# Stores moved to a second DMA ring, issued by ScalarE ten tiles behind the results

## The chip, the cores and the metric

One Trainium2 chip, one of its cores. The metric is the device time of one execution in microseconds (us); a median of several executions is quoted. Engine names: TensorE (PE) does matmuls, VectorE (DVE) and ScalarE (ACT) elementwise work, SyncE (SP) issues transfers. A transfer that SyncE or ScalarE issues is put in that engine's own ring (queues q1 and q10 on the pages below), a waiting list of transfers; 16 DMA engines take work from the rings. PSUM is the memory that TensorE writes its results to.

## The reference

```python
batch, m, k, n = 16, 512, 1024, 768
x          # (16, 512, 1024) float32
weight     # (1024, 768)     float32
sub_value  # (16, 512, 768)  float32
return (np.matmul(x, weight) - sub_value).astype(np.float32)
```

The 8192 rows of x are cut into 64 tiles of 128 rows ("m tiles"). Per tile 512 KB of x and 384 KB of sub_value are loaded and 384 KB of result are stored. With 3 MB of weight that is 87 MB in all.

## The kernel before

Two ring buffers live in on-chip memory: `x_ring` holds 16 tiles of x, `so_ring` holds 32 tiles of sub_value, in which the results replace what was subtracted. ScalarE casts a tile of x to 16 bits; TensorE transposes it (and ScalarE copies it out of PSUM), or, for the pairs of tiles in `ON_DVE`, VectorE transposes it; then TensorE multiplies, and VectorE subtracts. Tiles transposed by VectorE are cast seven tiles ahead of their matmuls, the others four.

All transfers are in one hand-ordered list, and SyncE issues them in that order: `x`, `w`, `s` are loads of x, weight and sub_value, `o` is a store; the numbers are the first tile and how many.

```python
TRANSFERS = [
    # ... the first 18 entries cut ...
    ('x', 27, 5), ('o', 0, 8), ('s', 24, 8), ('x', 32, 8), ('s', 32, 8), ('o', 8, 8),
    ('x', 40, 8), ('s', 40, 8), ('x', 48, 8), ('o', 16, 8), ('o', 24, 8), ('s', 48, 8),
    ('x', 56, 8), ('s', 56, 8), ('o', 32, 8), ('o', 40, 8), ('o', 48, 8), ('o', 56, 4),
    ('o', 60, 2), ('o', 62, 1), ('o', 63, 1),
]

def issue():                       # called after each cast and each subtraction
    while todo:
        kind, at, n = todo[0]
        # ... return if a buffer is not yet free, or a result not yet there (cut) ...
        todo.pop(0)
        # ...
        if kind == "o":
            keep(nc.sync.dma_start(out=there, in_=here))
        else:
            keep(nc.sync.dma_start(out=here, in_=there))

for mi in range(HEAD, n_mt):
    # ... matmuls of tile mi, transposes of tile mi + 2 (cut) ...
    for t in range(mi, n_mt):
        if t - lead(t) == mi:      # lead is 7 for tiles transposed by VectorE, else 4
            cast(t)
    finish(mi)                     # the subtraction
```

ScalarE runs its instructions in the order of the program, so a cast that waits for its load holds up everything behind it there. A load of sub_value into a place of `so_ring` must wait until the old result there has been stored. And in a single ring the list decides whose bytes move first: the transfers of the kernel before landed in the order of its list.

## Time and profile before

| | before |
|---|---|
| median time | 211.19 us of 3 runs, later 211.16 of 4 |
| span in the profile | 209.4 us |
| TensorE busy | 198.4 us |
| DMA engines busy | 97.7% of the span |
| bytes moved | 87.03 MB, 417 GB/s |
| last subtraction done, last store landed | 205.4, 208.5 us |

Read it from the outside in: two resources are above 90%, so first ask which of them the end hangs on (the chain that ended last says TensorE), then what the other one would do if it were a little later.

### The profile page before, as it was taken

How to read it: one execution, taken by the hardware profiler on the slowest of the kernel's cores; microseconds unless marked ns; L12 is line 12 of the kernel's file. 1: busy time of each engine (PE TensorE's matmuls, PEld its weight loads, DVE VectorE, ACT ScalarE, POOL GpSimd, SP SyncE). 2: the span in 40 equal slices, each digit the busy share in tenths (PEclk: the TensorE clock that was granted, in tenths of full speed). 3: DMA queues.
4: the chain of work that ended last, by engine and by line, in shares of the span. 5: the costliest groups of instructions: out<-in, count | busy, mean ns of one | idle time of the engine just before them, and what ended most of it. 6: DMA issues, size and time to landing. Idle time of an engine off the chain costs nothing.

```text
span 209.4 us, 2967 instructions
## 1 busy us (share of the span) xinstructions
PE 198.4 (95%) x1249; PEld 130.4 (62%) x1249; DVE 114.1 (54%) x186; ACT 112.6 (54%) x115; POOL 0.7 (0%) x6
## 2 busy tenths in 40 slices
PE   7998789999979999999999999999999999999990
PEld 2464467676656576676666666667666766766660
DVE  0342044206149849929946965992994795332231
ACT  3555565675396183655727629355573760765410
POOL 1000000000000000000000000000000000000000
PEclk9999999999999999999999999999999999999999
DMA  6999999999999999999999999999999999999994
GB/s 221 420 426 424 424 438 439 433 443 426 391 455 415 442 427 423 454 413 432 435 421 449 423 413 444 451 418 421 418 441 440 423 437 418 426 446 427 415 383 167
DMA packets 5629, 87.22 MB, mean 417 GB/s; under 512 B 624, under 2 KB 624, under 8 KB 2032
## 3 DMA queue, kind: packets, MB, share of 16 engines
q1 hardware_dynamic: 5616, 87.03, 97.7%
q8 instruction: 10, 0.16, 0.3%
q14 instruction: 3, 0.02, 0.0%
HBM read 61.87 MB, written 25.17 MB: 416 GB/s over the span
## 4 chain that ended last, share of the span: by engine, by line
PE 68%; DMA 20%; ACT 4%; DVE 3%; SPq 1%; issue 1%
PE psum_o L177 60%; DMA x_ring<-in_x_dram 20%; PE psum_t L144 8%; ACT x_tile L135 2%; DVE xtp_tile L165 2%; ACT xt_tile L151 1%; DVE so_ring L189 1%; SPq L110 1%; SPq L122 1%; ACT x16p_tile L132 0%
## 5 line engine op out<-in xcount | busy, mean ns | idle before, releaser
L177 PE MATMUL psum_o<-w_sb,xt_tile 128*128 128x384 f16 x800 | 145.7, 326 | 1.7 <-ACT xt_tile L151 1.1
L177 PEld LDWEIGHTS <-xt_tile 128*128 128x128 f16 x800 | 78.2, 98 | 41.5 <-ACT xt_tile L151 1.9
L189 DVE TENSOR_TENSOR so_ring<-psum_o,so_ring 128x768 f32<-128x768 f32 x64 | 60.7, 957 | 61.2 <-PE psum_o L177 41.1
L151 ACT COPY xt_tile<-psum_t 128x1024 f16<-128x1024 f16 x50 | 50.6, 1012 | 75.7 <-PE psum_t L144 74.9
L165 DVE STREAM_TRANSPOSE xtp_tile<-x16p_tile 32x256 f32<-32x256 f32 x112 | 48.8, 436 | 18.9 <-ACT x16p_tile L132 17.2
L144 PE MATMUL psum_t<-ident,x_tile 128*128 128x128 f32 x200 | 52.5, 275 | 2.8 <-ACT x_tile L135 2.4
L135 ACT CAST x_tile<-x_ring 128x1024 f16<-128x1024 f32 x50 | 51.6, 1049 | 5.5 <-DMA x_ring<-in_x_dram 5.5
L177 PE MATMUL psum_o<-w_sb,xtp_tile 128*128 128x384 f16 x224 | 42.9, 326 | 0.3 <-DVE xtp_tile L165 0.3
L144 PEld LDWEIGHTS psum_t<-ident,x_tile 128*128 128x128 f32 x200 | 27.8, 142 | 16.8 <-ACT x_tile L135 4.7
L177 PEld LDWEIGHTS <-xtp_tile 128*128 128x128 f16 x224 | 21.8, 98 | 10.4 <-DVE xtp_tile L165 0.7
L132 ACT CAST x16p_tile<-x_ring 128x1024 f16<-128x1024 f32 x14 | 14.6, 1046 | 5.8 <-DMA x_ring<-in_x_dram 4.7
L205 PE MATMUL psum_o<-idle_x,idle_w 128*128 128x512 f16 x25 | 8.8, 508 | 1.3 <-DVE idle_x L200 1.3
L112 DVE CAST w_sb<-so_ring 128x768 f16<-128x768 f32 x8 | 4.1, 556 | 10.5 <-DMA so_ring<-in_weight_dram 10.5
L205 PEld LDWEIGHTS <-idle_w 128*128 128x128 f16 x25 | 3.0, 120 | 5.0 <-issue 3.2
L135 ACT ACT_TABLE_LOAD x1 | 1.3, 1283 | 0.7 <-PEq L277 0.7
L199 DVE MEMSET idle_w<- 128x64 uint32 x1 | 0.1, 112 | 0.8 <-PEq L277 0.8
masks.py:199 POOL TENSOR_SCALAR_AFFINE_SELECT ident<-ident 128x128 f32<-128x128 f32 x1 | 0.3, 292 | 0.1
L200 DVE MEMSET idle_x<- 128x256 uint32 x1 | 0.3, 272 | 0.0
masks.py:197 POOL MEMSET ident<- 128x128 f32 x1 | 0.2, 205 | 0.3 <-POOLq L277 0.3
L277 POOL MEMSET const-bfloat16-1.0<- 128x1 bf16 x1 | 0.1, 101 | 0.0
L277 POOL MEMSET const-uint8-127<- 128x1 uint8 x1 | 0.1, 101 | 0.0
L277 POOL MEMSET const-float32-0.0<- 128x1 f32 x1 | 0.1, 98 | 0.2 <-issue 0.2
(1 smaller groups left out, 0.1 us busy)
## 6 DMA issues: line engine op xcount, KB each, us to landing
so_ring<-in_sub_value_dram SPq DMA_DIRECT2D x7, 3072.0 KB, 24.2
out_dram<-so_ring SPq DMA_DIRECT2D x7, 3072.0 KB, 31.2
x_ring<-in_x_dram SPq DMA_DIRECT2D x5, 4096.0 KB, 22.3
x_ring<-in_x_dram SPq DMA_DIRECT2D x2, 2560.0 KB, 23.3
x_ring<-in_x_dram SPq DMA_DIRECT2D x3, 1536.0 KB, 19.8
so_ring<-in_weight_dram SPq DMA_DIRECT2D x4, 768.0 KB, 8.7
x_ring<-in_x_dram SPq DMA_DIRECT2D x3, 512.0 KB, 6.2
so_ring<-in_sub_value_dram SPq DMA_DIRECT2D x1, 1536.0 KB, 22.2
```

Of the source, the lines that this page charges most:

```text
L110: keep(nc.sync.dma_start(out=st, in_=w_c[at]))
L112: keep(nc.vector.tensor_copy(out=w_sb[:, at, r], in_=st[:, r]))
L122: keep(nc.sync.dma_start(out=here, in_=there))
L132: keep(nc.scalar.copy(out=x16_t["pair", first][:, mi - first], in_=x_in))
L135: keep(nc.scalar.copy(out=x16_t[mi], in_=x_in))
L144: keep(nc.tensor.transpose(ps_t[mi].bitcast(F32)[:, c * P : (c + 1) * P], x16_t[mi].bitcast(F32)[:, c * P : (c + 1) * P], ident,))
L151: keep(nc.scalar.copy(out=xt_t[mi], in_=ps_t.pop(mi)))
L165: keep(nc.vector.transpose(xt[b * Q : (b + 1) * Q, :, a * Q : (a + 1) * Q], x16[a * Q : (a + 1) * Q, :, b * Q : (b + 1) * Q],))
L177: keep(nc.tensor.matmul(po_t[mi][:, h, :NS], xt_t[mi][:, 2 * P * c + r : 2 * P * (c + 1) : 2], w_sb[:, c, r, h * NS : (h + 1) * NS], start ...
L189: keep(nc.vector.tensor_tensor(out=o, in0=po_t.pop(mi)[:, :, :NS], in1=o, op=mybir.AluOpType.subtract))
L205: keep(nc.tensor.matmul(idle_o[:, 0], idle_w, idle_x, start=True, stop=True))
L277: nc = _bacc.Bacc("TRN2", target_bir_lowering=False, num_devices=1)
```

## The change

The intent is that the 16 DMA engines take from two rings at once: loads stay on SyncE's, stores go to ScalarE's. So that ScalarE need not wait for a subtraction before it can issue a store, each store is issued about ten tiles after its last result was due (tiles 0 to 7 after tile 18, for instance); near the end it trails by less.

```diff
-TRANSFERS = [
+LOADS = [
     # ... (loads in the same order, the 'o' entries taken out)
 ]
+STORES = [(18, 0, 8), (26, 8, 8), (34, 16, 8), (42, 24, 8), (50, 32, 8), (54, 40, 8),
+          (58, 48, 8), (61, 56, 4), (63, 60, 2), (63, 62, 1), (63, 63, 1)]
 ...
+    def store(at, n):
+        assert set(range(at, at + n)) <= done["finish"]
+        done["o"] |= set(range(at, at + n))
+        keep(nc.scalar.dma_start(
+            out=out_s[at // S][:, at % S : at % S + n], in_=so_ring[:, at % NSO : at % NSO + n]
+        ))
+        issue()
 ...
         del waiting[:PER]
+        for after, at, n in STORES:
+            if after == mi:
+                store(at, n)
```

An entry (34, 16, 8) means: after tile 34's part of the program, store the 8 tiles from 16 on.

## The prediction

> **What bounds the kernel now.** I read the page's busy shares first, then the 40 slices, the DMA queues, the chain that ended last, the queue's own waits, and last the trace's record of when each transfer was issued and landed.
>
> ```profile
> PE 198.4 (95%) x1249; PEld 130.4 (62%) x1249; DVE 114.1 (54%) x186; ACT 112.6 (54%) x115; POOL 0.7 (0%) x6
> ...
> DMA  6999999999999999999999999999999999999994
> ...
> q1 hardware_dynamic: 5616, 87.03, 97.7%
> ...
> PE 68%; DMA 20%; ACT 4%; DVE 3%; SPq 1%; issue 1%
> ```
>
> Two resources are full at once: TensorE is busy for 198.4 of 209.4 us, and one queue keeps the 16 DMA engines busy for 97.7% of the span. The chain ends on TensorE: from 70.7 us to 204.5 us it is an unbroken run of matmuls and transposes, then one subtraction of 0.96 us, then the last store, issued at 205.5 and landed at 208.5. All gaps of TensorE together are 4.8 us, all but about 0.3 us of them before 60 us. So nothing that touches only transfers after 60 us can shorten the TensorE part; it can only keep it or delay it.
>
> The transfers have no spare rate either. Landings follow each other like this: a 3 MB load or store (8 tiles of 384 KB, 3.146 million bytes) every 7.23 to 7.33 us, so 429 to 435 GB/s, and a 4 MB x load every 9.7 us, 432 GB/s. Loads and stores cost the same per byte. By tile, x, sub_value and output together are 1280 KB, 3.03 us of DMA at 432 GB/s, while TensorE takes about 2.89 us per tile (subtraction of tile 25 at 97.0 us, of tile 49 at 166.4: 69.4/24). DMA is therefore the slower of the two in steady state, and TensorE is never starved after 60 us only because the list of transfers puts urgent loads ahead and lets stores pile up: the last load lands at 177.9 us, and 12.6 MB of stores follow it.
>
> How tight this is shows on ScalarE and in the queue's waits:
>
> ```profile
> 122.21 1.04 ACT L132 CAST x16p_tile<-x_ring 128x1024 f16<-128x1024 f32 x1 [1.50 <-DMA x_ring<-in_x_dram]
> ...
> 139.22 1.05 ACT L132 CAST x16p_tile<-x_ring 128x1024 f16<-128x1024 f32 x1 [1.17 <-DVE xtp_tile L165]
> 143.33 1.01 ACT L151 COPY xt_tile<-psum_t 128x1024 f16<-128x1024 f16 x1 [3.07 <-PE psum_t L144]
> ```
>
> ```profile
> SPq L122 <- ACT x_tile L135: 75.2, 7, 22.4
> SPq L120 <- DVE so_ring L189: 47.0, 6, 20.9
> SPq L122 <- DMA out_dram<-so_ring: 46.9, 4, 24.4
> ```
>
> The first fence is ScalarE's timeline: the cast of tile 42 waited for x(40..47), which landed at 122.14, and the cast of tile 48 began at 139.22, 0.08 us after x(48..55) landed at 139.14. The view names VectorE, whose transposes free the buffer at about the same moment, but the load leaves no margin either. The second is what the sequencer of SyncE waits for: buffers to be free and results to be done. Those waits cost nothing now, because a deep backlog stands in the ring meanwhile.
>
> **What the Trainium skill says.** "DMA: Bandwidth & Descriptors", section "Issuing engines are not separate DMA queues": transfers issued from ScalarE and SyncE run on the same 16 engines, and issuing from several saves only the sequencer's issue time. Here an issue is 0.33 to 0.47 us, 39 times, and hidden. The same page, "Where 436 GB/s comes from", gives 435 GB/s as the ceiling of the fabric; the trace, at 429 to 435, agrees and leaves nothing for a second ring to fill. The same page, "Queues, rings and completion order", says that each engine goes round robin between rings that have work, packet by packet. The trace before has one data ring, so it shows this only faintly: the ten 16 KB packets of the instruction queue took 1.00 to 1.10 us each, against 0.63 us at the 26 bytes per ns of the data queue's packets, so they shared their engine.
>
> **The change part by part.**
> 1. Issues move: 11 stores at about 0.4 us, 4.4 us in all, go to ScalarE, which has 97 us idle. Trailing by ten tiles, they do not wait for the subtraction. Cost on the path: about 0.
> 2. No store is ahead of a load in a ring any more, and none behind. A store, once issued, takes every second packet. Packets are 24 KB for sub_value and output and 32 KB for x (one partition's row), so loads get about half of the rate while a store is in flight, wherever the store stood in the old order.
> 3. The order of bytes is what changes. I walk it with 7.3 us per 3 MB and 9.7 us per 4 MB. Up to 73.6 us (x 27..31 lands) it is unchanged. Then the bytes of store 0..7, sub 24..31 and x 32..39 are the same 24.3 us in either order, so x 32..39 still lands near 97.9. Store 8..15 (after tile 26, about 100 us), sub 32..39 and x 40..47 are again 24.3 us: x 40..47 still lands near 122.1. Now the difference. Before, sub 40..47 and x 48..55 came next, then store 16..23. In the changed kernel store 16..23 is issued after tile 34's part of ScalarE's program, about 120 us, so it shares the ring time with these two loads: 3+3+4 MB from 122.1 on, and x 48..55, the last to be issued, lands at about 146.4 in place of 139.1. That is **7.3 us late**, one store.
> 4. What this costs: the cast of tile 48 then begins at 146.5. ScalarE is in order, so behind it the copy of transposed tile 44 (143.33 before) starts at 147.5 and ends at 148.5. TensorE needs it at 146.17, where its first matmul on a copied tile after the pair 42 and 43 begins. Stall: 148.6 - 146.2 = **2.4 us**; the other 4.9 us are slack (3.07 us idle on ScalarE, 1.83 us from copy to use).
> 5. Later loads: x 56..63 has the same bytes ahead as before (about 170.7), wanted by a cast at about 175. Sub 56..63 must wait for store 24..31, which ScalarE, held by the cast of tile 48, issues only at about 150; it lands near 182 and is needed at 187. No stall there, little margin.
> 6. The tail: TensorE ends at 204.5 + 2.4 = 206.9. Store 48..55 is issued after tile 58 (191.0 + 2.4 = 193.4) into an idle ring; with 2.7 us from issue to full flow (the first 512 KB landed 3.96 us after issue, of which 1.25 is data) it lands at 203.4. Store 56..59 waits for tile 61, about 202.6, so the engines idle about 2 us, and data flow from 204.7. The last eight tiles (3 MB) land at 204.7 + 7.3 + 0.7 = 212.7, while the last subtraction, 207.9, plus 3.0 would allow 210.9. So the end trails TensorE by 5.8 us in place of 4.0: **1.8 us more**.
> Sum: 2.4 + 1.8 = 4.2 us, 208.5 to 212.7. On 211.19 us this is 215.4. I add 0.4 us, a guess, for rings that interleave less cleanly than one: **215.8 us**.
>
> **The rivals.**
> - Two rings move more than one: a read and a write side by side. For it: nearly all stretches of now move in one direction only, so no trace shows a mixed one. Against it: the rate is already at the page's ceiling, and loads and stores reach it alone. With 5% more in mixed stretches, some 20 us of mixing before 146 gives 1 us back on the stall and more elsewhere, about 213.5; with 10% the stall vanishes and only the tail is left, about 212.5. Faster by 2% (207) would need TensorE to end earlier, which it can't: its gaps lie before any store.
> - Two rings move less, through switching or through a less equal share. If loads got less than half, or mixing cost 5%, x 48..55 would be 2 to 3 us later, all of it stall: 218. With 10%, the cast of tile 42 would also stall: 221.
> - The transfer is hidden anyway: ScalarE has slack and loads get their bytes in time, within 1 us of before. It would need x 48..55 at 141.5 or earlier. Against it: that leaves 19.4 us after 122.1 for 24.3 us of bytes, unless x 40..47 lands clearly before 122. That can happen only if store 8..15 falls well behind, and it is issued 20 us ahead.
> - ScalarE stalls on its own issues, as a store waits for an earlier transfer on the same semaphore (eight are used in turn). I went through the order: the transfer eight earlier has landed in every case.
>
> **Range and chances.** 212.0 us is the tail cost alone with no stall; 220.5 is a loss of about 8% in mixed stretches. The 2% limit is 215.4, next to my sum. I think a loss of rate somewhat likelier than a gain, and the time lies a little above the limit: slower 0.55, within 2% 0.43, faster 0.02.
>
> **What would show it.** Step 2: two hardware_dynamic queues on the page, 61.9 and 25.2 MB, and sub 40..47 in flight for about 15 us or more instead of 7. Step 3: x 40..47 landing near 122 us, x 48..55 near 146. Step 4: one gap of TensorE of 2 to 3 us near 146 to 149 us, released by ScalarE's copy of the transposed tile, and the cast before it released by the DMA of x. Step 6: DMA slices below 9 near 190 and 203 us, and 5 to 6 us from the last matmul to the last landing. The prediction is wrong if mixed slices run clearly above 435 or below 415 GB/s, if x 48..55 lands before 142, or if stalls appear at other tiles.

## The result

The changed kernel took 216.49 us (216.07 to 217.24, 4 runs) against 211.16 us (210.99 to 211.29, 4 runs). The ratio is 1.0262, with a 95% interval of 1.0236 to 1.0287: slower by 2.6%. A ratio here is the mean time of one kernel's fast runs over that of the other's fast runs of the same rounds, so it is not quite the ratio of the medians. The outputs are right.

From the page of the changed kernel: busy times, two of the slice rows (40 equal slices of the span), the DMA queues, and the engines' shares of the chain that ended last.

```profile
PE 199.6 (93%) x1249; PEld 130.7 (61%) x1249; DVE 113.9 (53%) x186; ACT 112.3 (52%) x115; POOL 0.7 (0%) x6
...
PEclk9999999999999999999999999999799999999999
DMA  6999999999999999999999999999999999995877
...
q1 hardware_dynamic: 4032, 61.87, 68.8%
q10 hardware_dynamic: 1584, 25.17, 27.5%
...
PE 54%; DMA 32%; ACT 6%; DVE 3%; issue 2%; SPq 2%; ACTq 0%
```

There are two data queues now, and together they are busy for 96.3%. DMA has a larger part of the chain that ended last (32% in place of 20%). The new piece of that chain is one load of x, 27.16 us from 120.79 on, so the end now hangs on it. One slice of TensorE's clock is at 7 tenths, and the DMA engines are no longer full near the end.

The trace's record of landings shows where the order came apart (times in us; these are from the record of issues and landings, not a view of the page):

```
transfer          before: issued  landed     changed: issued  landed
x    40..47               96.32   122.14              96.37   125.52
store 16..23             121.12   146.46             117.96   136.99
sub  40..47              112.56   129.44             119.50   138.24
x    48..55              120.74   139.14             120.79   147.95
```

x 48..55 was issued at the same moment in both, and landed 8.8 us later. It did not run much beside the store itself: its packets start at 135.6, and the store landed at 137.0. The store had slowed x 40..47 and sub 40..47, which stand before it in the loads' ring. ScalarE's timeline shows what hung on it. The columns are start, duration, engine, line, operation, and in square brackets the idle time before it and what ended it:

```profile
125.60 1.04 ACT L133 CAST x16p_tile<-x_ring 128x1024 f16<-128x1024 f32 x1 [4.84 <-DMA x_ring<-in_x_dram]
...
148.03 1.04 ACT L133 CAST x16p_tile<-x_ring 128x1024 f16<-128x1024 f32 x1 [9.92 <-DMA x_ring<-in_x_dram]
148.13 0.34 ACTq L120 DMA_DIRECT2D out_dram<-so_ring  x1
148.98 1.01 ACT L152 COPY xt_tile<-psum_t 128x1024 f16<-128x1024 f16 x1
```

The second cast is that of tile 48. Before, it began at 139.22; now ScalarE stood still for 9.92 us until 148.03, and the copy behind it, of transposed tile 44, started at 148.98 in place of 143.33. TensorE, in the same stretch, first the beginning of tile 44 in the kernel before, then the changed kernel:

```profile
146.17 0.81 PE L177 MATMUL psum_o<-w_sb,xt_tile 128*128 128x384 f16 x4
```

```profile
150.04 1.46 PE L178 MATMUL psum_o<-w_sb,xt_tile 128*128 128x384 f16 x4 [3.65 <-ACT xt_tile L152]
151.30 0.42 PE L145 MATMUL psum_t<-ident,x_tile 128*128 128x128 f32 x1
151.51 1.45 PE L178 MATMUL psum_o<-w_sb,xt_tile 128*128 128x384 f16 x4
152.79 0.28 PE L145 MATMUL psum_t<-ident,x_tile 128*128 128x128 f32 x1
152.91 0.81 PE L178 MATMUL psum_o<-w_sb,xt_tile 128*128 128x384 f16 x4
```

TensorE waited 3.65 us for that copy; this is the only new gap of the whole run (8.7 us of gaps in all, in place of 4.8). And the eight matmuls after the gap took 1.46 and 1.45 us per four, where four take 0.81 us at full clock: that is the slice with 7 tenths. Tile 44 began at 150.04 in place of 146.17, 3.87 us late, and with about 1.4 us from the slow matmuls TensorE was 5.2 us late from there to the end: the last subtraction ended at 210.66 in place of 205.44. The last store landed 2.9 us after it, as before (3.1).

Did two rings change the rate? The view of windows, before and changed, columns after the window: its length, busy us of each engine, granted clock, DMA share, and last GB/s. First the kernel before:

```profile
95.00:102.00 7.00, 7.00 (x48) 4.71 (x46) 6.75 (x14) 3.84 (x5) 0.00 (x0) 1.00 1.00 427
102.00:116.00 14.00, 14.00 (x92) 9.47 (x91) 9.49 (x17) 8.18 (x9) 0.00 (x0) 1.00 1.00 429
```

Then the changed kernel:

```profile
95.00:102.00 7.00, 7.00 (x47) 4.74 (x46) 6.75 (x14) 3.84 (x5) 0.00 (x0) 1.00 0.99 341
102.00:116.00 14.00, 14.00 (x93) 9.43 (x91) 9.49 (x17) 8.23 (x9) 0.00 (x0) 1.00 1.00 426
```

From 102 to 116 us a load and a store ran side by side in the changed kernel, and the sum was 426 GB/s against 429 with one ring: mixing gains nothing and costs next to nothing. From 128 to 134 us I summed the packets by queue: 223 to 227 GB/s for the loads (then packets of sub 40..47 alone), 206 to 210 for the store. The dip at 95 to 102 us is another thing, to which I return: almost only loads ran there (the store's first packet starts at 101.6).

### The profile page after: what moved, and what is told of

The parts are those of the page before. It is cut to its first block, busy times and chain, and to the rows that moved or that the text cites. A ratio compares the mean times of both kernels' runs of the same rounds, so it can differ in the third digit from the quotient of the medians.

```text
span 214.4 us, 2970 instructions
## 1 busy us (share of the span) xinstructions
PE 199.6 (93%) x1249; PEld 130.7 (61%) x1249; DVE 113.9 (53%) x186; ACT 112.3 (52%) x115; POOL 0.7 (0%) x6
## 4 chain that ended last, share of the span: by engine, by line
PE 54%; DMA 32%; ACT 6%; DVE 3%; issue 2%; SPq 2%; ACTq 0%
PE psum_o L178 47%; DMA x_ring<-in_x_dram 32%; PE psum_t L145 7%; ACT x_tile L136 3%; ACT xt_tile L152 2%; DVE xtp_tile L166 2%; DVE so_ring L190 1%; SPq L108 1%; ACT x16p_tile L133 1%; SPq L113 1%; ACTq L120 0%; ACTq L133 0%; ACTq L152 0%
## 5 line engine op out<-in xcount | busy, mean ns | idle before, releaser
L178 PE MATMUL psum_o<-w_sb,xt_tile 128*128 128x384 f16 x800 | 147.3, 328 | 5.4 <-ACT xt_tile L152 4.8
```

The source lines that it names most:

```text
L178: keep(nc.tensor.matmul(po_t[mi][:, h, :NS], xt_t[mi][:, 2 * P * c + r : 2 * P * (c + 1) : 2], w_sb[:, c, r, h * NS : (h + 1) * NS], start ...
```

## The experiments

**Theory A**: the loss is one load, x 48..55. Two rings share the rate, so a store takes about half of it from whatever load is at the head of the other ring; the loads behind that one come late too, and the order of the list no longer protects them. **Rival B**: a second ring costs something of its own. **Rival C**: the trailing costs, not the ring. **Theory D**: part of the loss is TensorE's slow clock after the gap. All eight kernels gave right results, and each was run in rounds with the kernel before: the first four on one chip, where that kernel took 210.97 us, the last four on another, where it took 211.16 us. Ratios are to the runs of the same rounds.

### One store moved (late16)

```diff
-(34, 16, 8)
+(40, 16, 8)
```

> Two rings kept, one store moved: store 16..23 is issued after tile 40 instead of 34, everything else as changed. Theory A (the loss is the one load x 48..55, which shared the ring time with this store): the store no longer takes bytes before x 48..55, which lands at 139 to 142 us instead of 147.95; no stall of TensorE near 150; 211 to 212.5 us. Rival B (two rings cost something of their own, in rate or in the tail): most of the 5.3 us stays, 214 to 217.

212.27 us (211.77 to 212.65), ratio 1.0058 (1.0039 to 1.0076). Two rings are kept, and some 4 of the 5.3 us are gone. x 48..55 landed at 141.00. ScalarE's timeline of this run:

```profile
141.08 1.05 ACT L133 CAST x16p_tile<-x_ring 128x1024 f16<-128x1024 f32 x1 [3.06 <-DMA x_ring<-in_x_dram]
143.30 1.01 ACT L152 COPY xt_tile<-psum_t 128x1024 f16<-128x1024 f16 x1 [1.17 <-PE psum_t L145]
```

The cast still waited for the load, but the copy behind it then waited for TensorE, not the other way round. TensorE had no new gap, and the last subtraction ended at 205.4, as before. Theory A holds; B is left with the remaining 0.6%, and in the trace that is all in the tail: the last store landed 4.1 us after its issue in place of 3.0.

### One ring, same trailing (one_ring)

```diff
-        keep(nc.scalar.dma_start(
+        keep(nc.sync.dma_start(
             out=out_s[...], in_=so_ring[...]
```

> The stores keep their places in program order (trailing by ten tiles) but go to the queue of SyncE, so there is one ring again. Theory A: the order of bytes puts store 16..23 ahead of x 48..55 in the one ring too, which lands at 146 to 148 us; stall of 3 to 5 us near tile 44; 215 to 217 us. Rival B (it is the second ring that costs): back to 211 to 212.

220.12 us (219.27 to 220.22), ratio 1.0433. So taking the second ring away made the changed kernel worse, against rival B, and both expected times were missed. x 48..55 landed at 151.5, and TensorE's gap was 7.4 us. The direction is theory A's, but the size is beyond what I had expected, and this window of the run says why:

```profile
119.00:126.00 7.00, 7.00 (x46) 4.53 (x45) 4.72 (x8) 2.67 (x4) 0.00 (x0) 1.00 0.57 202
```

The engines were 57% busy. SyncE stood before the load sub 40..47, which has to wait until store 8..15 has landed; that store was the last thing in the ring, so the ring ran dry, and the next load took 11.5 us from 122.3 on in place of 7.3. In the hand-ordered list another load stood between the two. With stores on a second ring, x 40..47 was still in flight when that store landed and kept the engines full. With the stores in this order, the second ring is therefore a help where a load waits for a store. The run changes more than the ring, as the loads' issues move too; the cleaner test of B is early_stores, below.

### Two rings, no trailing (no_trail)

This is the kernel before with one edit in `issue()`:

```diff
-                keep(nc.sync.dma_start(out=there, in_=here))
+                keep(nc.scalar.dma_start(out=there, in_=here))
```

> The kernel before with one edit: stores are issued by ScalarE at their old places in the list, without the trailing. Theory A (on two rings a store takes half of the rate at once and an order of the list no longer holds it back): stores 16..23 and 24..31 both run beside x 48..55, which lands at about 150 us, and store 0..7 runs beside x 16..23 and x 24..26; stalls near tiles 18 and 44; 217 to 222 us, worse than the changed kernel. Rival C (the trailing is what costs, and the second ring is harmless): 211 to 213.

221.34 us (220.80 to 221.42), ratio 1.0483: the worst of all. Beside store 0..7, x 16..23 landed 0.9 us later than in the kernel before and sub 16..23 7.6 us later; TensorE had gaps of 2.0 us at 59.5 (1.1 at that place before) and of 0.5 us at 76.2. At 154.2 us came one of 5.4 us: x 48..55 landed at 152.1, after stores 16..23 and 24..31 had shared the rate with the loads. This refutes rival C: on two rings the trailing is what keeps the loss small. That ScalarE, without the trailing, lost time by waiting for results before it could issue can be ruled out up to there: its first four store issues came 0.06 to 0.13 us after the start of a copy, and what those copies had waited for was TensorE's transposes.

The gap of 2.0 us is worth a look for theory D. TensorE had been without a gap for over 5 us before it, and yet its clock fell: first TensorE's timeline, then the window after the gap, where the granted clock (third from the end) is 0.61.

```profile
59.49 1.06 PE L177 MATMUL psum_o<-w_sb,xt_tile 128*128 128x384 f16 x4 [2.02 <-ACT xt_tile L151]
60.44 0.48 PE L144 MATMUL psum_t<-ident,x_tile 128*128 128x128 f32 x1
60.70 1.49 PE L177 MATMUL psum_o<-w_sb,xt_tile 128*128 128x384 f16 x4
```

```profile
59.40:62.00 2.60, 2.51 (x10) 1.22 (x11) 0.63 (x2) 2.60 (x4) 0.00 (x0) 0.61 1.00 430
```

The run also answers the hope behind the change. A second ring does not add rate; it takes away the list as the means of saying who goes first.

### The gap filled with idle matmuls (fill)

```diff
             po_t[mi] = psum_o_pool.tile([P, 2, 512], F32, name="psum_o")
+            if mi == 44:
+                for _ in range(16):
+                    keep(nc.tensor.matmul(po_t[mi][:, 0], idle_w, idle_x, start=True, stop=True))
```

> The changed kernel with 16 idle matmuls of 512 columns (about 3.45 us) put ahead of tile 44's first matmul, where TensorE waited 3.65 us. Result is right, they are overwritten. Theory D (about 1.4 us of the loss is the half-speed stretch after the gap: the first 8 matmuls took 1.46 and 1.45 us per four in place of 0.76): no half-speed stretch, clock 1.0, last subtraction about 1.4 us earlier, 214.8 to 215.4 us. Rival E (the slow stretch has nothing to do with the gap, or follows anyway): unchanged at 216.1 to 217.2.

215.40 us (214.91 to 215.53), ratio 1.0203, some 1.1 us below the changed kernel. The load was nearly as late as ever (147.1), but TensorE's timeline shows no slow matmuls after the idle ones:

```profile
145.83 3.62 PE L178 MATMUL psum_o<-idle_x,idle_w 128*128 128x512 f16 x16
149.28 0.81 PE L181 MATMUL psum_o<-w_sb,xt_tile 128*128 128x384 f16 x4
```

The last subtraction ended at 209.3, 1.3 us earlier than in the changed kernel's trace; 0.4 us of that lay before tile 44, so some 0.9 us are the clock's. So the slow stretch belonged to the gap, and theory D is right: a stall of 3.65 us cost about a third more than itself. "TensorE: Matmul & The Clock Gate" in the Trainium skill, section "Why this matters for your kernels", says to leave no idle gap above about 3 us between matmuls; this gap agrees, but no_trail shows that less can be enough: 2.02 us of gap were followed by the slow clock too.

### The early cast taken away (tile48_pe)

```diff
-ON_DVE = frozenset(range(18, 60, 6))
+ON_DVE = frozenset(range(18, 60, 6)) - {48}
```

> The changed kernel, but tiles 48 and 49 go through TensorE's transposes instead of VectorE's, so that the cast of tile 48 stands three tiles later in ScalarE's order and is wanted only at about 147 us. x 48..55 still lands at 147 to 148 us. Theory A (the load is late, and what makes it cost is the early cast that holds ScalarE's queue): no gap of TensorE near 150, but 8 more transposes (0.9 us): 211.8 to 213.2 us. Rival (the lateness costs anyway, or TensorE loses for another reason): 215.5 to 217.5.

211.84 us (211.78 to 212.38), ratio 1.0040. x 48..55 landed at 148.9, even later than in the changed kernel and than I had expected, and cost nothing: the first cast that needs it stood three tiles further back in ScalarE's order. The copy of tile 44 in this run:

```profile
143.25 1.01 ACT L152 COPY xt_tile<-psum_t 128x1024 f16<-128x1024 f16 x1 [5.28 <-PE psum_t L145]
```

It came at 143.25, as in the kernel before, with 5.28 us of slack ahead of it. The last subtraction ended at 206.2, 0.8 us later than before, which is the eight added transposes (0.11 us each). This shows the second half of the mechanism: a late load cost time only because a cast that was not yet needed by TensorE waited for it ahead of a copy that was.

### Last stores earlier (tail_early, late16_tail)

Both have `(58, 48, 8), (61, 56, 4)` changed to `(56, 48, 8), (60, 56, 4)`, the first in the changed kernel and the second in late16.

> The changed kernel with the stores of tiles 48..55 and 56..59 issued two and one tiles earlier (after 56 and 60). The prediction's step 6 (the stores queue up at the end because they are issued late, 1.8 us): 1 to 2 us faster, 214.7 to 215.5. Rival (the tail is bound by the last store alone, which landed 2.86 us after its issue): unchanged, 216.0 to 217.2.

216.37 us (215.89 to 217.13), ratio 1.0250: no change against 1.0262. The last store landed 2.31 us after its issue in place of 2.86, with nothing left ahead of it when its data flowed, which is all there was to win; in this trace it was offset, as the last subtraction ended 0.5 us later (211.1).

> late16 with the same two stores earlier. In late16 the ring was full without a break from 162 us to the end, and the last store landed 4.1 us after its issue. Rival to step 6 (bytes, not issue times, bind this tail): unchanged at 211.8 to 212.7 us. Step 6: 211.0 to 211.5.

212.86 us (211.62 to 213.55), ratio 1.0074 (1.0044 to 1.0105), which overlaps that of late16. The median missed both expected ranges. The four runs spread over 1.9 us, so a change of half a microsecond either way would not show. It does not support step 6 of the prediction.

### The stores placed anew (early_stores)

```diff
-(18, 0, 8), (26, 8, 8), (34, 16, 8), (42, 24, 8), ... (58, 48, 8), (61, 56, 4), (63, 60, 2)
+(14, 0, 8), (24, 8, 8), (40, 16, 8), (41, 24, 8), ... (56, 48, 8), (60, 56, 4), (62, 60, 2)
```

> A try to match or beat both: two rings, first two stores four and two tiles earlier (so that sub 32..39 is in the ring well before its turn and the slow packets at 95 to 102 us go away), store 16..23 after tile 40, store 24..31 after 41, the last ones earlier. If the remaining 1.3 us of late16 are that dip: 210.5 to 211.3, level with the kernel before. If two rings cost something of their own: 212 or more.

211.15 us (210.98 to 211.73, 5 runs) against 211.16, ratio 1.0005 (0.9992 to 1.0017): level with the kernel before, on two rings. The window in which the changed kernel dipped to 341 GB/s:

```profile
95.00:102.00 7.00, 7.00 (x47) 4.76 (x46) 6.75 (x14) 3.84 (x5) 0.00 (x0) 1.00 0.97 418
```

So the second ring has no cost of its own that shows, and no gain either. No version beat the kernel before: in this one the last subtraction ended at 205.3 and the last store landed at 208.3, and TensorE's run of matmuls up to there is the same as before. What is not isolated is which of the moved stores brought late16's last 0.5% back, as several were moved at once. late16_tail moved two of them and won nothing that shows; what is left are the first two stores, with which the dip went, and those of tiles 24..31 and 60..61.

## Why the prediction was right

The time (215.8 foretold, 216.49 measured) and the place were right. By its steps:

- **Step 1, issues**: right. Each store's issue took 0.34 us of ScalarE's queue and did not wait for a subtraction in the changed kernel before the tail.
- **Step 2, half the rate**: right, 223 to 227 against 206 to 210 GB/s side by side.
- **Step 3, x 48..55 late**: right in mechanism, a little too small. 146.4 was foretold, 147.95 measured. x 40..47 was put at 122.1 and landed at 125.5, for two reasons: store 16..23, issued at 117.96 and not at 120, already took bytes from it, and there was the dip at 95 to 102 us. late16 has the dip (348 GB/s there) but not this store, and there x 40..47 landed at 122.9: so the dip was worth about 0.8 us of the 3.4, the store the rest.
- **Step 4, the stall**: right in mechanism, mis-sized. 2.4 us were foretold; tile 44 began 3.87 us late. The difference is the 1.5 us by which the load was later. Then a term was missing: the slow clock after the gap, about 1.4 us, which fill showed. Together 5.2 us in place of 2.4.
- **Step 5, sub 56..63**: right. It landed at 185.0 (182 foretold), without a stall.
- **Step 6, the tail, 1.8 us**: wrong in size. It was not there: the end trailed the last subtraction by 2.9 us, in place of 3.1, and the last matmul by 3.9 us, where 5 to 6 were foretold. The engines did idle near 195 us, as foretold (a slice at 5 tenths), but that did not lengthen the tail. I had taken 2.7 us from issue to full flow from the first transfer of the run; at the end a 3 MB store landed 8.73 us after its issue, of which 7.28 us are data, so the overhead was 1.45 us. And store 56..59 was issued 0.7 us before the subtraction of tile 61 ended, not after it.
- **The sum**: 2.4 + 1.8 + 0.4 of guess = 4.6 us, against 5.3 measured (5.0 between the two traces). A stall that was too small by 2.8 us and a tail that was too large by 2.0 us nearly made up for each other, so the closeness of the total is partly luck.
- **Slips in the working**: the lower end of the range, 212.0, is called the tail cost alone, but 211.19 + 1.8 is 213.0. The landings were not quite as regular as said: store 32..39 landed 8.53 us after the load before it. Neither bears on the sum.

Of the rivals, "two rings move more" fell (426 against 429 GB/s), and "hidden anyway" fell because of the early cast alone: tile48_pe shows that with a later cast the same lateness is hidden.

Left open is the dip itself. It occurs where sub 32..39 was issued only 3.6 us before its turn (94.3, its turn at 97.9), and it went when that load was issued earlier; one_ring has a similar slow stretch after its ring ran dry. The DMA engines count as 99% busy in the dip, but their packets were slow: of the load packets of 24 KB that start in these 7 us, half took over 1.0 us and some up to 2.14, where before none took more than 0.92. A busy share alone does not show this. That fresh transfers start slower is suggested by this, not shown by a run that isolates it.

## What to carry to other kernels

The DMA engines here were already full, and a second ring added no rate (426 against 429 GB/s) and gave up the order of the bytes, so each store had to be timed against the loads that were urgent beside it. Look for the load with the least margin and for what stands behind its first user on an in-order engine: moving one store by six tiles, or one cast by three, was worth most of the loss (some 4.0 and 4.6 of the 5.3 us). And look at TensorE's clock after a stall: here gaps of 2.02 us and of 3.65 us and more brought half the clock for 3.4 us or longer, by the clock record of the traces, while the gaps of up to 1.4 us in the kernel before did not, so such a stall costs more than itself.

## What the Trainium skill lacked or had wrong

- "DMA: Bandwidth & Descriptors", section "Issuing engines are not separate DMA queues", says that issuing from several engines saves only sequencer time. That is right of the rate (426 against 429 GB/s), but lacks what else it does: the order of bytes changes, which cost 2.6% here and 4.8% without the trailing; and a second ring can keep the engines fed while a load waits for a store (with the same order of stores 216.49 us with it, 220.12 without, where the engines fell to 57%).
- The same page, section "Queues, rings and completion order", has the round robin between rings, and the trace agrees (223 to 227 and 206 to 210 GB/s). It does not draw the conclusion that a load beside a store takes much longer: sub 40..47 landed 12.7 us after the load before it, in place of 7.3 us.
- The same page, section "Anatomy of one DMA — SWDGE (gpsimd) path", has a fixed cost of about 2 us per transfer, for transfers issued from GpSimd; it has no such fit for those of ScalarE and SyncE. Here 384 KB issued by ScalarE on an empty ring landed after 2.32 us (the last store of no_trail), of which 0.91 us are data at 432 GB/s: about 1.4 us.
- No page that I read has the dip to 341 GB/s, with the engines 99% busy, where a load was issued just before its turn.
- "TensorE: Matmul & The Clock Gate" has the clock's fall after an idle gap. Here 3.65 us of gap cost about 1.4 us more, and full clock was back 2.9 us after the gap's end (150.04 to 152.91). Its limit of about 3 us is too high for this case: a gap of 2.02 us in no_trail was followed by a granted clock of 0.61 (59.4 to 62 us).
